# Instance normalisation of 1 GB on one core: three tiles that share their rows, with the blocks of a transfer 192 KB apart

## Chip, cores and metric

The kernel runs on one core of a Trainium2 chip. The metric is the time on the device in microseconds (us), lower is better. Each kernel is run several times; kernels that are compared ran in turn on the same chip. The kernel before takes 4961.82 us, median of 3 runs (4961.65 to 4961.88).

## The reference

```python
x = np.random.randn(256, 256, 4096).astype(np.float32)
mean = np.mean(x, axis=2, keepdims=True)
var = np.var(x, axis=2, keepdims=True)
return ((x - mean) / np.sqrt(var + eps)).astype(np.float32)      # eps = 1e-5
```

Every one of the 65,536 rows of 4096 floats (16 KB) is normalised by itself. So 1.07 GB must be read and as much written, and any assignment of rows to partitions gives the right result as long as loads and stores agree.

## The kernel before

The rows are cut into 128 tiles of 512 rows. A tile has 128 partitions with K = 4 neighbouring rows each (64 KB a partition, 8 MB a tile). Three buffers X[0..2] are used in turn. Loads and stores are all issued by the sync engine, on one queue; every load and store of the steady part moves a whole tile.

```python
P, K, BUFS, Q = 128, 4, 3, 3072
ntiles = n // (P * K)                                        # 128
x_t = x_flat.rearrange("(t p k) d -> t p k d", p=P, k=K)     # a tile is 8 MB in one piece
out_t = out_flat.rearrange("(t p k) d -> t p k d", p=P, k=K)
...
def vector_tile(s, ...):
    take(V, ld, 16)                              # wait for the load
    for r in range(r0, r0 + k):                  # row sums; scales the row by 1/d in place
        V.tensor_scalar(out=x[:, r, :], ..., accum_out=mean[s][:, r : r + 1]).then_inc(means, 1)
    ...                                          # 1/std, bias; then the scaling of the rows
        V.tensor_scalar(out=x[:, r, f], ..., scalar1=rstd, scalar2=nbias, ...).then_inc(dn, 1)
...                                              # ScalarE: sums of squares, roots, part of one row
def rows_of(ap, t):
    if isinstance(t, int):
        return ap[t]
    first, period, count, i = t                  # in the loop: tile first + period * i
    ap = ap[first : first + period * (count - 1) + 1 : period]
    return ap[bass.ds(i, 1)].rearrange("o p k d -> p (o k) d")

def store(s, t):
    take(S, done[s], K + 1)
    S.dma_start(out=rows_of(out_t, t), in_=X[s][:, :, :]).then_inc(stored[s], 16)

def load(s, t, wait=True):
    if wait:
        take(S, stored[s], 16)
    S.dma_start(out=X[s][:, :, :], in_=rows_of(x_t, t)).then_inc(loaded[s], 16)
...
with S.Fori(0, rounds) as i:
    for t in range(L0, L0 + BUFS):
        store(t % BUFS, (t, BUFS, rounds, i))
        load((t + 2) % BUFS, (t + 2, BUFS, rounds, i))
```

The first and the last tile are moved in two halves of two rows a partition.

Of the kernel before, what the change touches and what calls it, by code (L numbers as in the profile page):

```python
# [10 lines left out]
def kernel(  # L11
# [11 lines left out]
    P = 128  # L23
    K = 4
    BUFS = 3
    Q = 3072

    x_flat = x.flatten_outer_dims()
    out_flat = out.flatten_outer_dims()
    n, d = x_flat.shape  # L30
    assert n % (P * K) == 0 and d & (d - 1) == 0

    ntiles = n // (P * K)
    x_t = x_flat.rearrange("(t p k) d -> t p k d", p=P, k=K)
    out_t = out_flat.rearrange("(t p k) d -> t p k d", p=P, k=K)
    assert ntiles == 128

    half = K // 2

# [7 lines left out]
    X = [pool.tile([P, K, d], fp32, name=f"x{s}") for s in range(BUFS)]  # L47
# [8 lines left out]
    loaded = [nc.alloc_semaphore(f"loaded{s}") for s in range(BUFS + 1)]  # L56
    stored = [nc.alloc_semaphore(f"stored{s}") for s in range(BUFS + 1)]
# [8 lines left out]
    def take(engine, sem, count):  # L66
        engine.wait_ge(sem, count)  # L67
        engine.sem_clear(sem)  # L68

    V, A, S = nc.vector, nc.scalar, nc.sync  # L70

    def vector_tile(s, r0=0, k=K, ld=None, dn=None):

        x = X[s]
        ld = loaded[s] if ld is None else ld
        dn = done[s] if dn is None else dn
        own = 0

        def mine(instruction):
            nonlocal own  # L80
            own += 1
            return instruction.then_inc(own_v, 1)

        if ld:
            take(V, ld, 16)
        for r in range(r0, r0 + k):
            V.tensor_scalar(  # L87
                out=x[:, r, :], in0=x[:, r, :], scalar1=1.0 / d, scalar2=None, op0=ALU.mult, op1=ALU.add,
                accum_out=mean[s][:, r : r + 1],
            ).then_inc(means, 1)  # L90
        for b in range(r0, r0 + k, 2):
            c = slice(b, b + 2)
            final = b == r0 + k - 2
            if final:
                take(V, stds, (b - r0) // 2 + 1)
            else:
                V.wait_ge(stds, (b - r0) // 2 + 1)
            mine(V.reciprocal(out=rstd[s][:, c], in_=std[s][:, c]))  # L98
            V.wait_ge(own_v, own)
            mine(V.scalar_tensor_tensor(  # L100
                out=nbias[s][:, c], in0=mean[s][:, c], scalar=-1.0 / d, in1=rstd[s][:, c], op0=ALU.mult, op1=ALU.mult
            ))
            if final:
                take(V, own_v, own)
            else:
                V.wait_ge(own_v, own)
            if final:
                V.sem_inc(scaled, 1)
            for r in range(b, b + 2):
                c = slice(r, r + 1)  # L110
                f = slice(Q, d) if r == r0 + k - 1 else slice(0, d)
                V.tensor_scalar(  # L112
                    out=x[:, r, f], in0=x[:, r, f], scalar1=rstd[s][:, c], scalar2=nbias[s][:, c],
                    op0=ALU.mult, op1=ALU.add,
                ).then_inc(dn, 1)

    def scalar_tile(s, r0=0, k=K, ld=None, dn=None):

        x = X[s]
        dn = done[s] if dn is None else dn  # L120
        last = r0 + k - 1
        own = 0

        def mine(instruction):
            nonlocal own
            own += 1
            return instruction.then_inc(own_a, 1)

        for r in range(r0, last + 1):
            c = slice(r, r + 1)  # L130
            if own:
                A.wait_ge(own_a, own)
            if r == last:
                take(A, means, k)
            else:
                A.wait_ge(means, r - r0 + 1)
            mine(A.activation(  # L137
                out=junk, in_=x[:, r, :], func=AF.Square, bias=mean[s][:, c], scale=-float(d), accum_out=ss[s][:, c]
            ))
            if (r - r0) % 2:  # L140
                c = slice(r - 1, r + 1)
                if r == last:
                    take(A, own_a, own)
                else:
                    A.wait_ge(own_a, own)
                A.activation(  # L146
                    out=std[s][:, c], in_=ss[s][:, c], func=AF.Sqrt, bias=eps_tile, scale=1.0 / d**3
                ).then_inc(stds, 1)
        c = slice(last, last + 1)
        take(A, scaled, 1)  # L150
        A.activation(  # L151
            out=x[:, last, :Q], in_=x[:, last, :Q], func=AF.Identity, bias=nbias[s][:, c], scale=rstd[s][:, c]
        ).then_inc(dn, 1)

    def rows_of(ap, t):

        if isinstance(t, int):
            return ap[t]
        first, period, count, i = t
        ap = ap[first : first + period * (count - 1) + 1 : period]  # L160
        return ap[bass.ds(i, 1)].rearrange("o p k d -> p (o k) d")

    def store(s, t):
# [8 lines that stand above are left out]
    def half_of(h):  # L172
        return slice(h * half, (h + 1) * half)

    def second(sems, s, h):
        return sems[BUFS] if h else sems[s]

    def store_half(s, t, h):
        r = half_of(h)
        take(S, second(done, s, h), half + 1)  # L180
        S.dma_start(out=out_t[t][:, r, :], in_=X[s][:, r, :]).then_inc(second(stored, s, h), 16)

    def halves(tile_fn, s, first):
        for h in range(2):
            ld = second(loaded, s, h) if first or h == 0 else False
            tile_fn(s, h * half, half, ld, second(done, s, h))

    last = ntiles - 1
    rounds = (ntiles - 5) // BUFS
    L0 = 2  # L190

    with tc.tile_critical():  # L192
        for h in range(2):
            r = half_of(h)
            S.dma_start(out=X[0][:, r, :], in_=x_t[0][:, r, :]).then_inc(second(loaded, 0, h), 16)
        load(1, 1, wait=False)
        store_half(0, 0, 0)
        store_half(0, 0, 1)
        load(2, 2, wait=False)
        store(1, 1)  # L200
        take(S, stored[BUFS], 16)
        load(0, 3)
# [5 lines that stand above are left out]
        load(last % BUFS, last)  # L208
        store((last - 2) % BUFS, last - 2)
        store((last - 1) % BUFS, last - 1)  # L210
        store_half(last % BUFS, last, 0)
        store_half(last % BUFS, last, 1)
        for s in ((last - 2) % BUFS, (last - 1) % BUFS, last % BUFS, BUFS):
            take(S, stored[s], 16)

        V.memset(eps_tile, eps / d**2).then_inc(ready, 1)  # L216
        halves(vector_tile, 0, True)
        vector_tile(1)
        with V.Fori(0, rounds) as i:  # L219
            for j in range(BUFS):  # L220
                vector_tile((L0 + j) % BUFS)
        vector_tile((last - 2) % BUFS)
        vector_tile((last - 1) % BUFS)
        halves(vector_tile, last % BUFS, False)

        take(A, ready, 1)
        halves(scalar_tile, 0, True)
        scalar_tile(1)
        with A.Fori(0, rounds) as i:
            for j in range(BUFS):  # L230
                scalar_tile((L0 + j) % BUFS)
        scalar_tile((last - 2) % BUFS)
        scalar_tile((last - 1) % BUFS)
        halves(scalar_tile, last % BUFS, False)
# [35 lines left out]
```

## Time and profile before

| | before |
|---|---|
| time, median | 4961.82 us |
| VectorE busy | 3298.0 us, 66% |
| ScalarE busy | 2407.7 us, 49% |
| DMA, mean rate | 433 GB/s |
| VectorE waiting for loads | 1580.4 us |

The lines themselves stand in the prediction below. In a page of the profile, the rows of digits give the busy tenths of 40 equal slices of the run. The line "q1" gives packets, MB and the time of the packets as a share of what sixteen engines have. A line of a DMA issue ends with the median time in us from issue to landing. A line of a wait reads: who waited, for whom, us in total, times, longest us.

### The profile page before, as it was taken

How to read it: one execution, taken by the hardware profiler on the slowest of the kernel's cores; microseconds unless marked ns; L12 is line 12 of the kernel's file. 1: busy time of each engine (PE TensorE's matmuls, PEld its weight loads, DVE VectorE, ACT ScalarE, POOL GpSimd, SP SyncE). 2: the span in 40 equal slices, each digit the busy share in tenths (PEclk: the TensorE clock that was granted, in tenths of full speed). 3: DMA queues.
4: the chain of work that ended last, by engine and by line, in shares of the span. 5: the costliest groups of instructions: out<-in, count | busy, mean ns of one | idle time of the engine just before them, and what ended most of it. 6: DMA issues, size and time to landing. Idle time of an engine off the chain costs nothing.

```text
span 4960.2 us, 5938 instructions
## 1 busy us (share of the span) xinstructions
DVE 3298.0 (66%) x2049; ACT 2407.7 (49%) x1412; POOL 0.2 (0%) x4
## 2 busy tenths in 40 slices
DVE  6666666666666666666666666666666666666666
ACT  4455444554445544455445544455444554445544
POOL 0000000000000000000000000000000000000000
DMA  9999999999999999999999999999999999999999
GB/s 422 431 435 433 431 435 433 432 437 432 432 438 432 433 437 432 433 437 432 435 435 432 436 434 431 438 433 431 438 433 432 438 432 433 438 432 433 438 432 405
DMA packets 37298, 2147.52 MB, mean 433 GB/s; under 512 B 4144, under 2 KB 4144, under 8 KB 4144
## 3 DMA queue, kind: packets, MB, share of 16 engines
q1 hardware_dynamic: 37296, 2147.50, 100.0%
q14 instruction: 2, 0.02, 0.0%
HBM read 1073.74 MB, written 1073.74 MB: 433 GB/s over the span
## 4 chain that ended last, share of the span: by engine, by line
DVE 62%; another core or an unknown queue 31%; issue 4%; DMA 2%; ACT 0%; DVEq 0%; ACTq 0%; SPq 0%
DVE x L87 44%; DVE x L112 17%; DMA x<-in_x_dram 1%; DVE nbias L100 1%; DMA out_dram<-x 1%; DVE rstd L98 1%; ACT junk L137 0%; DVEq L68 0%; DVEq L219 0%; ACT L146 0%; ACT std L146 0%; ACTq L68 0%; ACTq L67 0%; SPq L265 0%
## 5 line engine op out<-in xcount | busy, mean ns | idle before, releaser
L87 DVE TENSOR_SCALAR_CACHE_REDUCE x<-x 128x4096 f32<-128x4096 f32 x512 | 2232.3, 4416 | 1580.4 <-DMA x<-in_x_dram 1580.4
L137 ACT ACTIVATE junk<-x,mean 128x4096 f32<-128x4096 f32 x512 | 1883.1, 3678 | 2367.2 <-DVE x L87 2367.2
L112 DVE TENSOR_SCALAR x<-x,rstd,nbias 128x4096 f32<-128x4096 f32 (+1 forms) x512 | 1004.2, 2004 | 33.9 <-DVE nbias L100 29.3
L151 ACT ACTIVATE x<-x,nbias,rstd 128x3072 f32<-128x3072 f32 x130 | 383.2, 2948 | 146.2 <-DVEq L68 146.2
L137 ACT ACTIVATION_READ_ACCUMULATOR junk<-x,mean 128x1 f32 x512 | 95.5, 187 | 0.0
L146 ACT ACTIVATE std<-ss,eps_tile 128x2 f32<-128x2 f32 x256 | 75.6, 295 | 19.1
L98 DVE RECIPROCAL rstd<-std 128x2 f32<-128x2 f32 x256 | 40.7, 159 | 19.4 <-ACT std L146 19.4
L100 DVE SCALAR_TENSOR_TENSOR nbias<-mean,rstd 128x2 f32<-128x2 f32 x256 | 41.1, 161 | 8.9
L87 DVE DVE_READ_ACCUMULATOR x<-x 128x1 f32 x512 | 42.3, 83 | 0.0
L137 ACT ACT_TABLE_LOAD x1 | 1.3, 1283 | 1.2 <-DVE eps_tile L216 1.2
L146 ACT ACT_TABLE_LOAD x1 | 1.3, 1283 | 0.1
L216 DVE MEMSET eps_tile<- 128x1 f32 x1 | 0.1, 59 | 1.0 <-SPq L192 1.0
L251 POOL MEMSET const-bfloat16-1.0<- 128x1 bf16 x1 | 0.1, 101 | 0.0
L251 POOL MEMSET const-uint8-127<- 128x1 uint8 x1 | 0.1, 101 | 0.0
L251 POOL MEMSET const-float32-1.0<- 128x1 f32 x1 | 0.1, 99 | 0.0
L251 POOL MEMSET const-float32-0.0<- 128x1 f32 x1 | 0.1, 98 | 0.2 <-issue 0.2
## 6 DMA issues: line engine op xcount, KB each, us to landing
out_dram<-x SPq DMA_DIRECT2D x4, 4096.0 KB, 19.6
x<-in_x_dram SPq DMA_DIRECT2D x2, 4096.0 KB, 16.7
x<-in_x_dram SPq DMA_DIRECT2D x127, 50.3
out_dram<-x SPq DMA_DIRECT2D x126, 31.5
```

The lines of the kernel that those rows point to most:

```text
L87: V.tensor_scalar(out=x[:, r, :], in0=x[:, r, :], scalar1=1.0 / d, scalar2=None, op0=ALU.mult, op1=ALU.add, accum_out=mean[s][:, r : r + 1 ...
L98: mine(V.reciprocal(out=rstd[s][:, c], in_=std[s][:, c]))
L100: mine(V.scalar_tensor_tensor(out=nbias[s][:, c], in0=mean[s][:, c], scalar=-1.0 / d, in1=rstd[s][:, c], op0=ALU.mult, op1=ALU.mult))
L112: V.tensor_scalar(out=x[:, r, f], in0=x[:, r, f], scalar1=rstd[s][:, c], scalar2=nbias[s][:, c], op0=ALU.mult, op1=ALU.add,).then_inc(dn, 1)
L137: mine(A.activation(out=junk, in_=x[:, r, :], func=AF.Square, bias=mean[s][:, c], scale=-float(d), accum_out=ss[s][:, c]))
L146: A.activation(out=std[s][:, c], in_=ss[s][:, c], func=AF.Sqrt, bias=eps_tile, scale=1.0 / d**3).then_inc(stds, 1)
L151: A.activation(out=x[:, last, :Q], in_=x[:, last, :Q], func=AF.Identity, bias=nbias[s][:, c], scale=rstd[s][:, c]).then_inc(dn, 1)
L216: V.memset(eps_tile, eps / d**2).then_inc(ready, 1)
L251: nc = _bacc.Bacc("TRN2", target_bir_lowering=False, num_devices=1)
```

## The change

The intent is to give a tile's transfer on the memory side one dimension of 128 separate blocks, instead of one solid run of 8 MB. Tiles 0 and 1 stay. The other 126 form 42 groups of three that share 24 MB: a partition owns twelve neighbouring rows, and each of the three tiles takes four of them. A block is still four rows, 64 KB, but the next partition's block is 192 KB on.

```diff
-    x_t = x_flat.rearrange("(t p k) d -> t p k d", p=P, k=K)
-    out_t = out_flat.rearrange("(t p k) d -> t p k d", p=P, k=K)
     assert ntiles == 128
+    L0 = ntiles % BUFS
+
+    def by_tiles(ap):
+        groups = ap[L0 * P * K :].rearrange("(i p s k) d -> s i p k d", p=P, s=BUFS, k=K)
+        rest = ap[: L0 * P * K].rearrange("(t p k) d -> t p k d", p=P, k=K)
+        return groups, rest
+
+    x_t, out_t = by_tiles(x_flat), by_tiles(out_flat)
...
-    def rows_of(ap, t):
-
+    def rows_of(tiles, t):
+
+        groups, rest = tiles
         if isinstance(t, int):
-            return ap[t]
+            return rest[t] if t < L0 else groups[(t - L0) % BUFS][(t - L0) // BUFS]
         first, period, count, i = t
-        ap = ap[first : first + period * (count - 1) + 1 : period]
+        assert period == BUFS
+        first -= L0
+        ap = groups[first % BUFS][first // BUFS : first // BUFS + count]
         return ap[bass.ds(i, 1)].rearrange("o p k d -> p (o k) d")
... (the half transfers use rows_of too; L0 = 2 is no longer written as a number)
```

More of the change, by code (lines that the diff above doesn't have):

```diff
@@ L180, in store_half @@
         take(S, second(done, s, h), half + 1)
-        S.dma_start(out=out_t[t][:, r, :], in_=X[s][:, r, :]).then_inc(second(stored, s, h), 16)
+        S.dma_start(out=rows_of(out_t, t)[:, r, :], in_=X[s][:, r, :]).then_inc(second(stored, s, h), 16)
     def halves(tile_fn, s, first):
@@ L189 @@
     rounds = (ntiles - 5) // BUFS
-    L0 = 2
     with tc.tile_critical():
@@ L194 @@
             r = half_of(h)
-            S.dma_start(out=X[0][:, r, :], in_=x_t[0][:, r, :]).then_inc(second(loaded, 0, h), 16)
+            S.dma_start(out=X[0][:, r, :], in_=rows_of(x_t, 0)[:, r, :]).then_inc(second(loaded, 0, h), 16)
         load(1, 1, wait=False)
```

## The prediction

> **What bounds the kernel now.** I read the busy tenths of the page first, because they show whether any engine is full, and then the DMA queue and the DMA issues, because only the DMA row is full.
>
> ```profile
> span 4960.2 us, 5938 instructions
> DVE 3298.0 (66%) x2049; ACT 2407.7 (49%) x1412; POOL 0.2 (0%) x4
> ...
> DMA  9999999999999999999999999999999999999999
> ...
> DMA packets 37298, 2147.52 MB, mean 433 GB/s; under 512 B 4144, under 2 KB 4144, under 8 KB 4144
> ...
> q1 hardware_dynamic: 37296, 2147.50, 100.0%
> ...
> x<-in_x_dram SPq DMA_DIRECT2D x127, 50.3
> out_dram<-x SPq DMA_DIRECT2D x126, 31.5
> ```
>
> The reader is to see three things. VectorE is busy two thirds of the time and ScalarE half, while the DMA digit is 9 in every one of the 40 slices. The one queue used fills 100.0% of sixteen engines' span. And a full load takes 50.3 us from issue to landing although its 8.39 MB need only 8.39 MB / 433 GB/s = 19.4 us: it stands in line behind other transfers, so the queue is not starved.
>
> The longest waits of the engines agree with this, since VectorE, the first engine in a tile's work, waits for loads:
>
> ```profile
> DVE x L87 <- DMA x<-in_x_dram: 1580.4, 126, 13.2
> ```
>
> That is 1580.4 / 126 = 12.5 us of spare time per tile on VectorE. A tile's period is 2 x 19.4 = 38.7 us (one load and one store), and consecutive store issues around 2000 us are indeed 38.5 to 38.9 us apart. The sync queue also shows a long wait, for VectorE's last scaling, but that is the pacing of the stores and it does not leave the DMA idle: when a store is issued at 2009.40 us in the timeline, the next load is still arriving (its first reader starts at 2021.72 us). So the DMA has about 12 us of queued work at every store issue. I take the chain of waits, which puts 62% on VectorE, as misleading here, for it follows instructions and names the transfers only as "another core or an unknown queue 31%".
>
> The windows of the steady part show the same full DMA:
>
> ```profile
> 50.00:2000.00 1950.00, 1304.57 (x807) 948.79 (x557) 0.00 (x0) 1.00 1.00 434
> 2193.00:4800.00 2607.00, 1736.90 (x1082) 1263.17 (x743) 0.00 (x0) 1.00 1.00 434
> 4940.00:4960.20 20.20, 1.60 (x2) 1.44 (x1) 0.00 (x0) 1.00 0.62 264
> ```
>
> Columns after the stretch are its length, the busy times of VectorE, ScalarE and GpSimd, clock, DMA share and GB/s. Only the last 20 us have a DMA share well below 1.
>
> **The packets themselves.** The trace's packet records hold 32,384 data packets of 64 KB and 768 of 32 KB (the six half transfers at the two ends), and 4,144 of 4 bytes (259 transfers x 16 engines: the completions). A 64 KB packet takes 2418 ns at the median and 2420.2 ns in the mean; 99% lie at 2432 ns or below. A 32 KB packet takes 1213 ns at the median, 1226.5 in the mean, a completion 9.0 ns. Summed per engine: 2024 x 2.4202 = 4898.4 us, 48 x 1.2265 = 58.9 us, 259 x 0.009 = 2.3 us, together 4959.6 us. With 2 us ahead of the first packet and 1 us behind the last, less a few microseconds by which records overlap, this is the whole span of 4960.2 us. The kernel is a stream of packets at a constant duration.
>
> [...]
>
> **The change part by part.** It removes nothing and adds nothing in instructions. Tiles 0 and 1 stay as they are (128 mod 3 = 2). The other 126 tiles form 42 groups of 24 MB; in a group, partition p owns twelve neighbouring rows, and slot s takes four of them. So:
> - Number of transfers: 259 before, 259 after. Bytes: 2 x 1073.74 MB before and after.
> - Size of a contiguous block: four rows of 16 KB = 64 KB in memory and 64 KB in a partition, as before. Only the distance between blocks goes from 64 KB (a transfer is one solid 8 MB) to 192 KB (a transfer is 128 blocks in 24 MB). Packets should stay at 64 KB, cost 0.
> - Compute on the tiles: the same shapes, 0. Address arithmetic on the sync sequencer changes slightly; issues now take 0.34 to 0.35 us, four register steps cost some 0.03 to 0.04 us each, and about 12 us of queued work stand in front, so even a doubling is hidden: 0.
> - Row pitch in HBM: this is the only real question. 192 KB is 3 x 64 KB. Modulo 8 MB, multiplying by the odd number 3 only permutes the 128 slots of 64 KB: the 128 blocks fall once on each slot, as before. [...] Cost: 0, with an allowance of a few microseconds.
>
> The sum is 0. I add 1 us[...]: **4963.0 us**, against 4961.8.
>
> **Rivals.** *First, the memory serves blocks 192 KB apart worse than a solid run.* For it: [...]the packets have almost no room, so anything slower lands in full on the time. Against it: the pitch is not a power of two, and each block still has 64 KB in a row. Each 1% on the mean packet is 24 ns x 2024 = 49 us; a 2% loss of time needs a mean of about 2469 ns. I give a visible loss under 2% some 8%, and over 2% some 4%. *Second, the broken-up memory side makes the packets smaller,* for instance one row of 16 KB. Two packets of 32 KB cost 2 x 1213 = 2426 ns against 2418, so 8 ns for one more packet. Four packets of 16 KB are three more, 24 ns: 2024 x 24 ns = 49 us, an estimate of 5010 us. Against it: four rows are still contiguous on both sides, as in the 32 KB halves, where two rows already move as one packet. About 5%. *Third, the new placing is kinder to the memory and the time falls.* The whole excess of the mean packet over the median is 2.2 ns x 2024 = 4.4 us[...]. *Fourth, VectorE becomes the bound.* It does the same work with 12.5 us to spare per tile; nothing speaks for it.
>
> **Range and chances.** The low end is the removal of all stragglers, about 4957 us. The high end allows 0.4% on the packets, about 4982 us; the runs of before agree within 0.3 us, so noise adds nothing. Outside lie the second rival and the larger cases of the first. Faster by over 2% would need 16 engines at 442 GB/s[...]: 0.01. Slower by over 2%: 0.04. Within 2%: 0.95.
>
> **What would show it.** Right: 37,296 packets on the queue, none between 512 B and 8 KB, a 64 KB packet near 2418 ns, 433 GB/s, DMA digits all 9, VectorE 3298 us busy and waiting some 12.5 us per tile. The first rival would show as a mean packet above 2430 ns with VectorE's wait for loads grown by the same time, the second as some 130,000 packets, the third as a mean at 2418 ns. [...]

The forecast's sum: 0 for every part, plus an allowance of 1 us, on 4961.8 us; that is 4962.8 us, stated as 4963.0 us. The allowance is worked out from no measurement. For the row pitch the arithmetic of the 128 slots stands; that only the power of two in a pitch matters was the assumption, and no run had yet shown another pitch than 64 KB. What stands on measurements is the 4.4 us of the third rival, and the 0.01 for a gain of over 2% was the author's estimate. The median packet, 65,536 B in 2418 ns, gives 433.7 GB/s on sixteen engines.

## The result

The changed kernel takes 4962.51 us (median of 4 runs, 4961.88 to 4962.93), the kernel before beside it 4961.85 us (4 runs, 4961.65 to 4962.58). The ratio is 1.0001, with a 95% interval of 0.9984 to 1.0018: the same. A ratio is the mean time of one kernel's fast runs over that of the other's of the same rounds, so it is not quite the ratio of the medians.

The page of the changed kernel, its parts on busy time, DMA and issues:

```profile
span 4961.1 us, 5938 instructions
DVE 3297.9 (66%) x2049; ACT 2407.5 (49%) x1412; POOL 0.2 (0%) x4
...
DMA  9999999999999999999999999999999999999999
...
DMA packets 37298, 2147.52 MB, mean 433 GB/s; under 512 B 4144, under 2 KB 4144, under 8 KB 4144
...
q1 hardware_dynamic: 37296, 2147.50, 100.0%
...
x<-in_x_dram SPq DMA_DIRECT2D x127, 50.3
out_dram<-x SPq DMA_DIRECT2D x126, 31.6
```

Its waits, and two of the stretches that the prediction showed (length, busy VectorE, ScalarE, GpSimd, clock, DMA share, GB/s):

```profile
DVE x L95 <- DMA x<-in_x_dram: 1581.5, 126, 13.4
```

```profile
50.00:2000.00 1950.00, 1304.97 (x809) 948.85 (x557) 0.00 (x0) 1.00 1.00 434
2193.00:4800.00 2607.00, 1736.38 (x1082) 1262.81 (x741) 0.00 (x0) 1.00 1.00 434
```

The reader is to see that it is the same profile, line by line: the same number of packets, none of a new size, the same rate, the same wait of 12.5 us per tile. The packet records agree: 64 KB packets have a median of 2418 ns and a mean of 2420.1 ns, before 2418 and 2420.2.

A "same" alone does not say why. The prediction rests on three statements that this pair of runs cannot test: that a pitch of 192 KB is harmless because 3 is odd, that a packet more costs 8 ns, and that VectorE has 12.5 us to spare. Twelve experiments took them apart.

### The profile page after: what moved, and what is told of

The parts are those of the page before. It is cut to its first block, busy times and chain, and to the rows that moved or that the text cites. A ratio compares the mean times of both kernels' runs of the same rounds, so it can differ in the third digit from the quotient of the medians.

```text
span 4961.1 us, 5938 instructions
## 1 busy us (share of the span) xinstructions
DVE 3297.9 (66%) x2049; ACT 2407.5 (49%) x1412; POOL 0.2 (0%) x4
## 2 busy tenths in 40 slices
DMA packets 37298, 2147.52 MB, mean 433 GB/s; under 512 B 4144, under 2 KB 4144, under 8 KB 4144
## 3 DMA queue, kind: packets, MB, share of 16 engines
q1 hardware_dynamic: 37296, 2147.50, 100.0%
## 4 chain that ended last, share of the span: by engine, by line
DVE 62%; another core or an unknown queue 31%; issue 4%; DMA 2%; ACT 0%; DVEq 0%; ACTq 0%; SPq 0%
DVE x L95 44%; DVE x L120 17%; DMA x<-in_x_dram 1%; DVE nbias L108 1%; DMA out_dram<-x 1%; DVE rstd L106 1%; ACT junk L145 0%; DVEq L76 0%; DVEq L229 0%; ACT L154 0%; ACT std L154 0%; ACTq L76 0%; ACTq L75 0%; SPq L275 0%
```

## The experiments

In what follows, "the packets" are the trace's records of single DMA packets. Where runs of one kernel fall into two groups, it is said. By the rule of 2%, e2, e3, e5, e9, e10 and e12 count as the same as the kernel before and e4 as unclear; losses below 2% are called losses here only where the run's times and the lower group of before beside it do not overlap.

### 1. The pitch: power of two, or distance (e1 and e2)

e1 is the kernel before with all 128 tiles sharing all rows, so that blocks lie exactly 8 MB apart:

```diff
-    x_t = x_flat.rearrange("(t p k) d -> t p k d", p=P, k=K)
+    x_t = x_flat.rearrange("(p t k) d -> t p k d", p=P, k=K)     # out_t in the same way
```

> All 128 tiles share all the rows: partition p owns 512 neighbouring rows, so the 128 blocks of 64 KB of one transfer lie exactly 8 MB apart, and all start at the same place modulo 8 MB. Theory A (what made 192 KB harmless is that it is an odd multiple of 64 KB, so that the 128 blocks fall on 128 different slots modulo 8 MB): here that protection is gone, and the transfers slow down clearly[...], with a 64 KB packet well above 2418 ns. Rival B (blocks of 64 KB in one run make any pitch harmless[...]): 4962 us within 0.3%, packet median 2418 ns.

e2 is the changed kernel with one group of 127 tiles behind tile 0, blocks 8.1 MB apart:

```diff
-        groups = ap[L0 * P * K :].rearrange("(i p s k) d -> s i p k d", p=P, s=BUFS, k=K)
-        rest = ap[: L0 * P * K].rearrange("(t p k) d -> t p k d", p=P, k=K)
+        group = ap[P * K :].rearrange("(p s k) d -> s p k d", p=P, k=K)
+        rest = ap[: P * K].rearrange("(t p k) d -> t p k d", p=P, k=K)
...
+        first -= 1
+        ap = group[first : first + period * (count - 1) + 1 : period]
```

> 127 tiles share their rows: the blocks of a transfer lie 127 x 64 KB = 8.1 MB apart, as far as in e1 but an odd multiple of 64 KB. Theory A: as fast as before, 4962 us, packet 2418 ns. Rival B: the same. Rival C (the distance itself costs[...]): as slow as e1, whatever that is; if e1 is slow and this is not, it is the power of two and not the distance.

e1 took 7049.82 us (4 runs, 7042.7 to 7064.27), ratio 1.4192 (1.4116 to 1.4268). Page and waits of e1:

```profile
DMA  9999999999999999999999999999999999999999
...
DMA packets 37298, 2147.52 MB, mean 305 GB/s; under 512 B 4144, under 2 KB 4144, under 8 KB 4144
...
q1 hardware_dynamic: 37296, 2147.50, 97.8%
...
x<-in_x_dram SPq DMA_DIRECT2D x127, 80.9
```

```profile
DVE x L87 <- DMA x<-in_x_dram: 3656.0, 127, 44.2
```

Page and waits of e2:

```profile
DMA packets 37298, 2147.52 MB, mean 433 GB/s; under 512 B 4144, under 2 KB 4144, under 8 KB 4144
...
x<-in_x_dram SPq DMA_DIRECT2D x127, 50.3
```

```profile
DVE x L95 <- DMA x<-in_x_dram: 1581.4, 126, 13.3
```

The same packets of the same size, the same DMA digits of 9, and yet 305 instead of 433 GB/s: in e1 the engines are busy, but a 64 KB packet takes 3358.9 ns in the mean. VectorE only waits longer for its loads. So a full row of 9 says that packets are under way, not that they move at the full rate; the GB/s says that.

e2 has two runs at 4963.56 and 4963.73 us and two at 5005.76 and 5006.3 us. The kernel before, on that chip, has five runs between 4960.84 and 4962.20 us and two at 5004.14 and 5006.36 us, so the pairs near 5005 us are not e2's own. Each group of e2 lies within 2 us of a group of before. Distance is not the cause (rival C falls), and blocks of 64 KB do not protect (rival B falls): at almost the same distance, 8 MB costs 42% and 127 x 64 KB costs nothing.

### 2. How much of a power of two (e5, e6, e11)

e5 and e6 share rows among 8 and 32 tiles (pitch 512 KB and 2 MB). Their tiles no longer follow each other at even distances, so the loop of the sync engine is written out and `rows_of` returns `ap[t]` (not shown):

```diff
+    x_g = x_flat.rearrange("(g p s k) d -> g s p k d", p=P, k=K, s=32)     # e5: s=8
+    x_t = [x_g[t // 32][t % 32] for t in range(ntiles)]                    # out_t in the same way
...
-        with S.Fori(0, rounds) as i:
-            for t in range(L0, L0 + BUFS):
-                store(t % BUFS, (t, BUFS, rounds, i))
-                load((t + 2) % BUFS, (t + 2, BUFS, rounds, i))
+        for t in range(L0, L0 + BUFS * rounds):
+            store(t % BUFS, t)
+            load((t + 2) % BUFS, t + 2)
```

> Groups of 8 tiles: blocks of a transfer 512 KB apart, so the 128 blocks fall on only 16 different places modulo 8 MB, eight blocks on each; the transfers are issued from an unrolled list instead of a loop. Theory A (a power of two takes places away; e1 showed 1.42 times the time at 8 MB): some loss[...]. Rival (only pitches of several MB are harmful[...]): 4962 us within 0.3%.

> Groups of 32 tiles: blocks 2 MB apart, four different places modulo 8 MB. Theory A: between e5 and e1[...]. If this is as slow as e1, 7050 us, the places above 2 MB do not matter; if it is 4962 us, only the step from 2 MB to 8 MB hurts.

e11 gives 96 tiles a pitch of 6 MB and leaves the last 32 tiles at 2 MB:

```diff
-    x_t = [x_g[t // 32][t % 32] for t in range(ntiles)]
+    x_a = x_flat[: 96 * P * K].rearrange("(p s k) d -> s p k d", p=P, k=K)
+    x_b = x_flat[96 * P * K :].rearrange("(p s k) d -> s p k d", p=P, k=K)
+    x_t = [x_a[t] if t < 96 else x_b[t - 96] for t in range(ntiles)]
```

> 96 tiles share rows with blocks 6 MB apart, which is 3 x 2 MB, the last 32 tiles as in e6 with 2 MB. Theory A in its sharp form (only the power of two in the pitch counts, an odd factor such as 3 merely permutes the places): as e6, 5522 us within 1%. Rival (what counts is how far apart the blocks are): between e6 and e1's 7050 us, near 6300 us. Rival (the factor 3 helps, as it may have at 192 KB): well below 5522 us.

| pitch | run | time, median us | ratio | mean 64 KB packet, ns |
|---|---|---|---|---|
| 64 KB | before | 4961.85 | 1 | 2420.2 |
| 192 KB | the change | 4962.51 | 1.0001 | 2420.1 |
| 512 KB | e5 | 4973.70 | 1.0001 | 2424.2 |
| 2 MB | e6 | 5522.16 | 1.1103 | 2680.9 |
| 6 MB, last quarter 2 MB | e11 | 5722.51 | 1.1532 | 2768.4 |
| 8 MB | e1 | 7049.82 | 1.4192 | 3358.9 |
| 127 x 64 KB | e2 | two groups, see above | 1.0046 | 2420.6 |

The pages of e5 and e6, in this order:

```profile
DMA packets 37302, 2147.55 MB, mean 432 GB/s; under 512 B 4144, under 2 KB 4144, under 8 KB 4144
```

```profile
DMA packets 37302, 2147.55 MB, mean 388 GB/s; under 512 B 4144, under 2 KB 4144, under 8 KB 4144
```

The ratio of e5 hides a small loss. Two of the seven runs of before beside it lay high (4992.62 and 5001.02 us); against the five others, 4961.88 to 4962.46 us, e5's four runs, 4971.77 to 4975.33 us, are some 11 us slower. By the packets most of it falls in the first 500 us, where the mean is 2472 ns against 2433 before. Whether the 11 us are due to the pitch or to the written-out loop was not separated. As e6 and e11 have the same written-out loop, it explains no more than some 11 us of their losses. The loss proper starts between 512 KB (4973.70 us) and 2 MB (5522.16 us).

e11 missed what theory A said of it: 5722 us is 3.6% over e6's 5522 us, though far from the 6300 us of the rival. But e11 ran on another chip than e6, and it carries its own control, the last 32 tiles. Windows of e11, the first within the 6 MB part, the second within the 2 MB part (columns as above):

```profile
50.00:4200.00 4150.00, 2398.26 (x1488) 1743.12 (x1023) 0.00 (x0) 1.00 0.99 375
4400.00:5650.00 1250.00, 723.49 (x449) 526.23 (x309) 0.00 (x0) 1.00 1.00 377
```

Within one execution, 6 MB runs at 375 GB/s and 2 MB at 377: 0.5% apart. e6 ran at 388 GB/s throughout. The last 32 tiles of e6 are the same rows in the same layout as those of e11, and there e6 ran at 390 GB/s (4250 to 5450 us) where e11 ran at 377. So the factor 3 neither helps nor hurts noticeably, and the 3% between e6 and e11 is between executions on two chips, of which the reason stays open. This supports the sharp form of theory A within e11, and it is the closest analogue of the change itself, where 192 KB is 3 x 64 KB.

### 3. Reads or writes (e7, e8)

e7 gives only the loads the pitch of 8 MB, e8 only the stores; the rows come out permuted. Their outputs are wrong, which doesn't matter for the times.

```diff
-    x_t = x_flat.rearrange("(t p k) d -> t p k d", p=P, k=K)
+    x_t = x_flat.rearrange("(p t k) d -> t p k d", p=P, k=K)     # e7; e8: out_t alone
```

> The loads take the 8 MB pitch of e1, the stores stay solid as before; the rows come out permuted, so the result is wrong on purpose. If reads and writes suffer alike, half of e1's loss of 2088 us: about 6005 us. If only reads suffer: about 7050 us; if only writes: 4962 us.

> The other half: the stores take the 8 MB pitch, the loads stay solid, the result is wrong on purpose. If reads and writes suffer alike about 6005 us; only writes: about 7050 us; only reads: 4962 us. The losses of e7 and e8 should add up to e1's 2088 us if the two do not disturb each other.

e7 took 5678.05 us (2 runs), e8 6049.94 us (2 runs). Waits of VectorE, first e7, then e8:

```profile
DVE x L87 <- DMA x<-in_x_dram: 2291.4, 127, 24.2
```

```profile
DVE x L87 <- DMA x<-in_x_dram: 2661.4, 126, 29.9
```

Both directions suffer, the stores more: against 4962.4 us the losses are 716 and 1088 us, together 1804 of e1's 2088 us. Neither "only reads" nor "only writes" holds. The remaining 284 us arise only when both have the pitch, or between chips (e1 ran on another one).

### 4. The size of a packet (e3)

e3 is the changed kernel with the letters s and k of the layout exchanged: the three tiles take the twelve rows of a partition in turn, so a block falls into four runs of 16 KB.

```diff
-        groups = ap[L0 * P * K :].rearrange("(i p s k) d -> s i p k d", p=P, s=BUFS, k=K)
+        groups = ap[L0 * P * K :].rearrange("(i p k s) d -> s i p k d", p=P, s=BUFS, k=K)
```

> The changed kernel with the rows dealt out in turn: a partition still has twelve neighbouring rows, but a tile takes every third one, so its block is four runs of 16 KB, 48 KB apart. It tests the rival on packet size. By the prediction's estimate of 8 ns for one more packet: some 130,000 packets of 16 KB at about 610 ns, 24 ns more for every 64 KB, about 5010 us (1.0% slower than the changed kernel). If the packets stay fully overlapped: 4963 us. If the memory dislikes the shorter runs: clearly over 5010 us.

Page of e3:

```profile
DMA packets 133939, 2147.52 MB, mean 430 GB/s; under 512 B 4145, under 2 KB 4145, under 8 KB 4145
...
q1 hardware_dynamic: 133936, 2147.50, 100.4%
```

It took 4997.68 us (4 runs, 4996.23 to 4999.77); ratio 1.0056, where the two high runs of before pull the ratio down. Against the lower group of before it is 35.6 us, where 49 were estimated. The median packet is 611 ns, so four are 26 ns longer than one of 64 KB, close to the estimated 24. The wall time rises less because records overlap: the share is 100.4% here. So packets matter as the prediction said, at three quarters of its size, and the change did not run into this because its block stayed in one run. A rival stays: e3 also asks the memory for runs of 16 KB, 48 KB apart, and no run separates that from the number of packets. What speaks for the packets is that 26 ns for three more of them fit the 8 ns for one more, which were read from the 32 KB packets at the ends of the kernel before.

### 5. VectorE's spare time (e4, e9, e12)

e4 and e9 put a useless pass (times 1) over four and over two rows of each tile ahead of the means in the changed kernel:

```diff
+        for r in range(r0, r0 + k):              # e9: k // 2
+            mine(V.tensor_scalar(
+                out=x[:, r, :], in0=x[:, r, :], scalar1=1.0, scalar2=0.0, op0=ALU.mult, op1=ALU.add
+            ))
+        V.wait_ge(own_v, own)
```

> The changed kernel with a useless multiplication by 1 of all four rows ahead of the means: 4 x 2.0 = 8.0 us more on VectorE per tile, 34 us of 38.7. If the DMA is the bound with 12.5 us to spare per tile, the time moves only by what stands bare at the two ends, at most about 10 us, to 4963 to 4975 us, VectorE busy about 4330 us, and its wait for loads falls from 1581 to about 550 us. If VectorE were on the path as the chain of waits says, it would be 128 x 8 = 1030 us slower, 5990 us.

> The changed kernel with the useless multiplication on two rows of four: by e4's 2.2 us each, 4.45 us more on VectorE per tile, leaving about 8 us of queued transfers when a store is issued, where e4 left 3.5 us and lost 1 us per tile. If a store issued with over about 5 us in front of it loses nothing: 4963 to 4970 us and no more than 7 us of idle DMA. If any cut into the 12.5 us costs (e4's loss of 125 us is proportional): about 5025 us.

e4 took 5087.7 us (4 runs, 5085.76 to 5089.47), ratio 1.0237 (1.0184 to 1.029); e9 5015.99 us (4 runs, 5011.1 to 5019.15), ratio 1.0106. Both misses: I had put them at 4963 to 4975 and 4963 to 4970 us. Page and waits of e4:

```profile
DVE 4437.5 (87%) x2561; ACT 2407.6 (47%) x1412; POOL 0.2 (0%) x4
...
q1 hardware_dynamic: 37296, 2147.50, 98.9%
...
x<-in_x_dram SPq DMA_DIRECT2D x127, 43.2
```

```profile
DVE x L96 <- DMA x<-in_x_dram: 575.1, 125, 12.1
```

A row of the pass took 2.29 us, not the 2.0 expected, so the delay is 8.9 us per tile. VectorE still waits 4.6 us per tile for loads and yet the kernel is 125 us slower, 1 us per tile. The rival in its plain form, VectorE as the bound with 1030 us more, is as wrong. For e9, the pass itself and the waits:

```profile
L95 DVE TENSOR_SCALAR x<-x 128x4096 f32<-128x4096 f32 x256 | 575.6, 2290 | 1068.0 <-DMA x<-in_x_dram 1068.0
```

```profile
DVE x L95 <- DMA x<-in_x_dram: 1068.0, 126, 11.9
```

4.5 us more work per tile, 8.5 us of wait left, 54 us lost. Either the delay costs, or the traffic of the passes in the on-chip memory slows the transfers. e12 tells these apart: the same delay without the traffic. (A pass over a row is 128 x 16 KB = 2 MB; the "512 KB-wide" of the expectation is a slip.)

```diff
+        for _ in range(22 * k // K):
+            mine(V.reciprocal(out=scratch, in_=scratch))      # 128x2
+            V.wait_ge(own_v, own)
... (scratch is a 128x2 tile, set to 1 once at the start)
```

> The changed kernel with a chain of 22 tiny reciprocals on two columns, each waiting for the one before, ahead of a tile's means: at the 0.20 us from one such instruction to the next in the trace about 4.4 us more on VectorE per tile, the same delay as in e9, but next to no traffic in the on-chip memory. It tells apart two readings of e9's loss of 54 us. If it is the delay (stores issued with less in the queue): as e9, 5011 to 5020 us, long packets at the changes between load and store. If it is the traffic of the 512 KB-wide passes that slows the DMA: 4962 to 4964 us.

It took 5017.44 us (4 runs, 5012.4 to 5021.16), ratio 1.0108. The waits of e12:

```profile
DVE scratch L96 <- DMA x<-in_x_dram: 1087.1, 126, 11.8
```

The same loss as e9, 55 us, so it is the delay. It is not the second level near 5005 us: beside e9 all nine runs of before lie at 4960.96 to 4963.12 us, beside e12 seven of eight at 4961.77 to 4963.02. Two things worked out from the records show where it bites. The first is how far apart the sixteen completions of one transfer land, median over the transfers of the steady part; the second is the mean 64 KB packet by the time since the last store was issued:

```
                                        changed     e9       e12
first to last completion, us              7.4    6.0-6.5   6.2-6.8
mean packet starting  4-6 us, ns          2421      2511      2516
                      8-10                2423      2418      2418
                      18-20               2418      2574      2680
                      22-24               2419      2418      2418
```

In the changed kernel the first completion of a transfer lands 7.4 us ahead of the last (5.9 us in e10, the same kernel, which was no slower); this gap grows from about 0.5 us to 6 us over the first few dozen transfers. Read as one completion for each of sixteen engines (the trace names no engine), this says that when a store is issued, the last engine still has about 12 us to do, but the first one only about 12.4 - 7.4 = 5 us, while the wait of VectorE, which is for the last of sixteen completions, does not tell of it. A delay of 4.5 us takes the first engine close to the edge. That this is why the delay costs is a reading that the runs do not show. Only two delays were tried, and the loss is nearly proportional to them: 54 us at 4.5 us per tile, 125 us at 8.9, that is 12 and 14 us for each us of delay. The rival in e9's expectation, that any cut into the 12.5 us costs (5025 us, measured 5016), is not ruled out, and no run shows a delay that is free.

The long packets of e9 and e12 lie at the changes from load to store and from store to load, and the mean over all is 2445 and 2446.9 ns; idle time in e9 is only some 11 us, 5 more than in the kernel before. Followed to the completion record behind it, a long packet is mostly the last of the eight that belong to one completion (chained end to start, the records of the changed kernel form sixteen lines, in which 4,023 of the 4,144 completions have eight packets of 64 KB before them): between 500 and 4800 us these last ones have a mean of 2609 ns in e9, 2625 in e12 and 2423 in the changed kernel, and they hold 40 of the 48 us per engine by which e9's packets exceed 2418 ns. But the engines closest to running out are not those whose load packets stretch: in e9 the last load packets that start in the 2 us before a store's issue keep 2418 ns, those that start 1 to 6 us after it take 2.85 to 3.0 us. Why a packet lasts longer once the queue is short, rather than merely starting later, these runs do not show.

### 6. The changed kernel again (e10)

The kernel is unaltered.

> The changed kernel itself, unaltered, against the kernel before on one chip, to narrow the interval of the main result. Expected by every theory: most runs at 4962 to 4963 us for both. On two other chips single runs of the kernel before and of e2 lay near 5000 to 5006 us; if that is a state of the chip and not of a kernel, the changed kernel should show it too in some runs.

It took 4962.06 us (5 runs, 4961.38 to 4963.61), before 4962.23 us (9 runs, 4960.96 to 4963.12), ratio 1.0 (0.9987 to 1.0014). On this chip neither kernel had a run near 5005 us, so whether the changed kernel can have one stays open. The kernel before had single runs at 5001 to 5013 us on three chips (5004.14, 5006.36, 5001.02 and 5012.56 us) and one at 4992.62 us, at the same clock of 1.0, while most lay at 4962 us. No profile caught one, so the cause is open.

## Why the prediction was right, point by point

- **The bound.** DMA at 433 GB/s, before and after; right. The trace of the change repeats 12.5 us of wait per tile and 2418 ns per packet.
- **Packets stay at 64 KB.** Right: 37,296 on the queue. e3 shows what the other case would have cost, 36 us rather than the 49 us of the second rival. Its term was sized too large: the 24 ns per 64 KB were about right (26 measured), but adding them up neglected that records overlap (a share of 100.4% in e3).
- **An odd multiple is harmless.** Right, and now tested: 127 x 64 KB costs nothing at 8.1 MB of distance (4963.56 us in its lower group), 8 MB costs 42%, and 6 MB equals 2 MB within 0.5% in one run. But at the change's own distance the odd factor may not have been needed: even 512 KB, a power of two, cost next to nothing (some 11 us), and 128 and 256 KB were not run. Why the power of two costs was not shown; only that it did from 2 MB on. That the prediction took 8 MB as the modulus is not confirmed as such either: 16 places (512 KB) cost 0.2% at most, four (2 MB) 11%, one (8 MB) 42%.
- **The first rival's size.** No measured figure stood behind its 8% and 4%; they were the author's estimate. That a pitch can cost is shown by the powers of two: the rate lost was about 0.2% at 512 KB (432 of 433 GB/s, pitch and written-out loop together), 10% at 2 MB (388 of 433) and 30% at 8 MB (305 of 433). At 192 KB it was nothing (433 GB/s).
- **No gain to be had.** Right: the means of the packets before and after differ by 0.1 ns.
- **VectorE's spare time of 12.5 us.** The change did not touch it, so the predicted time did not depend on it. But the statement that nothing speaks for the fourth rival was too easy: 4.5 us of delay already cost 1%. A wait that ends with the last of sixteen completions overstated what could be spent; that the spread between the engines is the reason is argued, not shown.
- **The allowance of 1 us.** 4963.0 was said, 4962.51 and 4962.06 were measured; the difference to before is within noise.

## What to carry to other kernels

Here the packets already ran at a constant duration (median 2418 ns, mean 2420.2), and another order of the same blocks gained nothing (mean 2420.1). Nothing was lost with blocks of 64 KB at 3 or 127 times 64 KB, but 11 to 42% when the pitch was a multiple of 2 MB (2, 6 and 8 MB), so of the groups tried here those with an odd number of tiles, 3 and 127, were the safe choice. Read GB/s and the mean packet beside the DMA's busy share, which stayed at 9 in e1 while 30% of the rate was gone (305 of 433 GB/s). And do not take the whole wait of an engine for its loads as free: here 4.5 of 12.5 us already cost 54 us, so try a delay before counting on it.
